# Lp pooling on one core: the blocks of x and out laid out in reverse order of work

## Chip, cores and metric

The kernel runs on one core of one Trainium2 chip; the other cores are idle. The metric is the device time of one launch in microseconds, the median of several runs. A profile is one further execution, taken by the hardware profiler.

## What is computed

The input x is 32 x 256 x 4096 float32 (134.22 MB), p is 2 and the window is 4. Each output element is the root of the mean of four squares that lie side by side, so out is 32 x 256 x 1024 float32 (33.55 MB):

```python
for i in range(length // 4):
    window = np.abs(x[:, :, 4*i:4*i + 4]) ** 2.0
    result[:, :, i] = np.mean(window, axis=-1) ** 0.5
```

A window never crosses the end of a row of x, and windows follow each other without a gap. So x and out can both be read as flat arrays: elements 4j to 4j+3 of x give element j of out, wherever they stand. Any cut of x into pieces whose length is a multiple of 4 gives a cut of out into pieces a quarter as long.

## The kernel before

**Blocks and tiles.** The flat x has 262,144 elements for each of the 128 partitions. This width is cut into 20 tiles (L41 to L47): 18 of 13,184 columns, tile 3 of 13,152, tile 19 of 11,680. The tiles are grouped into six blocks (L51): four of four tiles (0 to 3, 4 to 7, 8 to 11, 12 to 15), one that holds tiles 18, 16, 17 in this order of columns, and one of tile 19 alone. The widths of the blocks are 52,704, three times 52,736, 39,552 and 11,680.

**Where a block lies in memory.** A block is one unbroken stretch of the flat x. Within it, partition 0 owns the first `block_width` elements, partition 1 the next ones, and so on. The function `rows` (L64) computes where the stretch begins (L65), and views it as 128 rows (L66). It is used for x with `div` 1 (in `load`, L83) and for out with `div` 4 (in `store`, L86). With `sum(block_width[:b])`, block 0 is at the front of both arrays and block 5 at their end.

**Loads.** `load(i)` brings tile i, 13,184 columns of all 128 rows of its block, into one of three buffers xt (L58); it is issued by SP. The first three loads go out at the start (L122); load i + 3 goes out once tile i has been summed and its buffer is free (L144).

**Work on a tile.** ACT squares the tile in place (L89). DVE adds columns in pairs (L95) and the pairs into fours (L99), which end in the output tile ot, in PSUM (st), or, for the last tiles, in an xt buffer that is free. ACT takes the roots (L102). For tiles 18 and 19 DVE does a part of the squares (L155). The order of the instructions on each engine is written out by hand (a manual schedule from L62 on, with `ahead` and `behind` in L126 and L127 saying when the roots are taken).

**Stores.** A block is stored by one DMA when all its roots are there. Stores 0, 1 and 2 are issued by ACT (L116), so they have a DMA queue of their own beside the loads; stores 3, 4 and 5 are issued by SP (L147, L168, L172), behind all loads in the queue of the loads.

The functions that the edit touches:

Of the kernel before, what the change touches and what calls it, by code (L numbers as in the profile page):

```python
# [1 line left out]

# [4 lines left out]


@with_exitstack
def kernel(  # L10
    ctx: ExitStack,
    tc: tile.TileContext,
    x: bass.AP,
    p: float,
    kernel_size: int,
    out: bass.AP,
):

    nc = tc.nc

    assert float(p) == 2.0, "kernel specialized for p == 2"
    k = int(kernel_size)  # L30
    assert k == 4, "kernel specialized for kernel_size == 4"

    P = nc.NUM_PARTITIONS
    fp32 = mybir.dt.float32
    Act = mybir.ActivationFunctionType
    add = mybir.AluOpType.add
    xf = x.rearrange("b c l -> (b c l)")
    of = out.rearrange("b c l -> (b c l)")
    total = xf.shape[0] // P

    W = 13184  # L41
    R = W // k
    X_SLOTS = 3
    NARROW = W - 32
    LAST = total - 18 * W - NARROW
    widths = [W] * 3 + [NARROW] + [W] * 15 + [LAST]
    n = len(widths)  # L47
    assert 0 < LAST <= W and LAST % 16 == 0


    blocks = [[0, 1, 2, 3], [4, 5, 6, 7], [8, 9, 10, 11], [12, 13, 14, 15], [18, 16, 17], [19]]  # L51
    block_of = {i: b for b, group in enumerate(blocks) for i in group}
    block_width = [sum(widths[i] for i in group) for group in blocks]

    x_pool = ctx.enter_context(tc.tile_pool(name="x_pool", bufs=1))
    o_pool = ctx.enter_context(tc.tile_pool(name="o_pool", bufs=1))
    s_pool = ctx.enter_context(tc.tile_pool(name="s_pool", bufs=1, space=bass.MemoryType.PSUM))
    x_tiles = [x_pool.tile([P, W], fp32, name=f"xt{j}") for j in range(X_SLOTS)]  # L58
    o_tile = o_pool.tile([P, 4 * R], fp32, name="ot")
    first = o_pool.tile([P, 1], fp32, name="first")  # L60
    s_tile = s_pool.tile([P, 4096], fp32, name="st")
    ctx.enter_context(tc.manual_schedule())  # L62

    def rows(flat, b, div):  # L64
        at = sum(block_width[:b]) * P // div  # L65
        return flat[at:at + block_width[b] * P // div].rearrange("(p w) -> p w", p=P)  # L66


    free = x_tiles[17 % X_SLOTS]
    place = {i: o_tile[:, i % 4 * R:i % 4 * R + widths[i] // k] for i in range(16)}  # L70
    place[18] = free[:, R:2 * R]
    place[19] = free[:, 0:LAST // k]
    place[16] = free[:, 2 * R:3 * R]
    place[17] = free[:, 3 * R:4 * R]
    held = [o_tile[:, 0:w // k] for w in block_width[:4]] + [free[:, R:4 * R], place[19]]

    xs, loads, stores, sums, squares = {}, {}, {}, {}, {}

    def load(i):
        b = block_of[i]  # L80
        at = sum(widths[j] for j in blocks[b][:blocks[b].index(i)])
        xs[i] = x_tiles[i % X_SLOTS][:, 0:widths[i]]
        loads[i] = nc.sync.dma_start(out=xs[i], in_=rows(xf, b, 1)[:, at:at + widths[i]])  # L83

    def store(b, queue):
        stores[b] = queue.dma_start(out=rows(of, b, k), in_=held[b])  # L86

    def square(v):
        return nc.scalar.activation(out=v, in_=v, func=Act.Square)  # L89

    def pairs(v):

        q = v.rearrange("p (n j) -> p n j", j=k)
        h = v[:, 0:v.shape[1] // 2].rearrange("p (n j) -> p n j", j=2)
        return nc.vector.tensor_tensor(out=h, in0=q[:, :, 0:2], in1=q[:, :, 2:4], op=add)  # L95

    def fours(o, v):
        h = v[:, 0:v.shape[1] // 2].rearrange("p (n j) -> p n j", j=2)
        return nc.vector.tensor_tensor(out=o, in0=h[:, :, 0], in1=h[:, :, 1], op=add)  # L99

    def root(o, s):
        return nc.scalar.activation(out=o, in_=s, func=Act.Sqrt, scale=1.0 / k)  # L102

    summed = {i: s_tile[:, 0:R] if i in (4, 8, 12, 16) else place[i] for i in range(n)}

    def roots(*group):
        if len(group) == 1:
            root(place[group[0]], summed[group[0]])
        else:
            v = o_tile[:, group[0] % 4 * R:(group[-1] % 4 + 1) * R]  # L110
            r = root(v, v)
            if group[0] in (5, 9):

                implied(r, stores[block_of[group[0]] - 1])
        if group[-1] in (3, 7, 11):
            store(block_of[group[-1]], nc.scalar)  # L116

    def implied(later, earlier):

        tc.declare_no_dep(later.ins, earlier.ins, reason="implied by the other waits")  # L120

    for i in range(X_SLOTS):  # L122
        load(i)


    ahead = {4: (3,), 8: (7,), 12: (11,)}  # L126
    behind = {3: [(0, 1, 2)], 7: [(5, 6), (4,)], 11: [(9, 10), (8,)], 14: [(12,)], 15: [(13, 14)], 16: [(15,)]}  # L127

    root(first[:, :], nc.const_aps.tensor(1.0, (P, 1), fp32))
    for i in range(17):  # L130
        if i in ahead:
            roots(*ahead[i])
        s = square(xs[i])
        squares[i] = s
        if i == 3:
            implied(s, squares[0])
        if i in (3, 7, 11):

            for earlier in sums[i - X_SLOTS]:
                implied(s, earlier)  # L140
        for group in behind.get(i, []):
            roots(*group)
        sums[i] = pairs(xs[i]), fours(summed[i], xs[i])
        if i + X_SLOTS < n:  # L144
            load(i + X_SLOTS)

    store(3, nc.sync)  # L147
    square(xs[17])
    pairs(xs[17])
    fours(summed[17], xs[17])  # L150
    later = {18: 4608, 19: 2000}

    def shared_square(i):
        v = xs[i][:, 0:later[i]]
        nc.vector.tensor_tensor(out=v, in0=v, in1=v, op=mybir.AluOpType.mult)  # L155
        square(xs[i][:, later[i]:widths[i]])

    def shared_pairs(i):
        implied(pairs(xs[i]), loads[i])

    shared_square(18)
    roots(16)
    roots(17)
    shared_pairs(18)
    fours(summed[18], xs[18])
    shared_square(19)
    roots(18)
    store(4, nc.sync)  # L168
    shared_pairs(19)
    fours(summed[19], xs[19])  # L170
    roots(19)
    store(5, nc.sync)  # L172


# [1 line left out]
_INS = ['x', 'p', 'kernel_size']  # L176
_OUTS = [((32, 256, 1024), 'float32')]

_NUMBERS = {'p': 2.0, 'kernel_size': 4}


# [26 lines left out]
```

## Time and profile before

| what | value |
|---|---|
| median of 3 runs | 393.82 us (393.79, 393.82, 394.0) |
| span of the profiled execution, first to last instruction | 392.3 us |
| median less this span | 1.5 us |
| busy: DVE, ACT, POOL | 218.2, 274.4, 0.2 us |
| moved by DMA | 167.77 MB, mean 428 GB/s over the span |
| one load of 13,184 columns | 6,592 KB, 29.8 us from issue to landing (median of 18) |
| one square (L89) of 13,184 columns | 11.19 us |
| pairs and fours (L95, L99) of such a tile | 7.03 and 3.59 us |

The profile has no total of its own for the profiled execution; its span is the time that a sum can be made against, and what lies around it is taken from the runs. The engines' queues are named ACTq and SPq. DMA q1 is the queue of SP, q10 that of ACT. Beside its page, the trace holds a record for every packet that a DMA engine moved: a packet is here the piece of one partition's row that a load or a store moves, 52,736 bytes in most loads.

### The profile page before, as it was taken

To read this page: it belongs to the slowest core of one execution; us is meant where nothing else is said; L and a number is where in the kernel's file an instruction comes from. 1 tells how busy PE (TensorE), PEld (TensorE's weight loads), DVE (VectorE), ACT (ScalarE), POOL (GpSimd) and SP (SyncE) were. 2 spreads that over 40 slices of the span, in tenths; PEclk is the share of its full clock that TensorE was granted. 3 is DMA by queue.
4 is the path that set the end of the run, shared out by engine and by line. 5 is a ranking of instruction groups with operands and counts; after the bars stand their busy time and mean duration, and the time that the engine had idled before them with its cause. 6 is when DMAs were issued, how large, how long until landed. Compare 5 with 4: busy or idle time off the path is not lost.

```text
span 392.3 us, 176 instructions
## 1 busy us (share of the span) xinstructions
DVE 218.2 (56%) x42; ACT 274.4 (70%) x37; POOL 0.2 (0%) x4
## 2 busy tenths in 40 slices
DVE  0009477580693274905942748069418485699970
ACT  1095695979950859799509597995098999969910
POOL 0000000000000000000000000000000000000000
DMA  8999999999999999999999999999999999999997
GB/s 344 430 430 430 430 440 435 452 457 366 430 430 430 430 430 430 430 441 446 452 446 441 436 430 436 430 430 430 430 430 430 430 430 430 430 453 415 430 413 342
DMA packets 3744, 167.77 MB, mean 428 GB/s; under 512 B 416, under 2 KB 416, under 8 KB 416
## 3 DMA queue, kind: packets, MB, share of 16 engines
q1 hardware_dynamic: 3312, 147.53, 87.4%
q10 hardware_dynamic: 432, 20.25, 11.9%
HBM read 134.22 MB, written 33.55 MB: 428 GB/s over the span
## 4 chain that ended last, share of the span: by engine, by line
DMA 43%; ACT 30%; DVE 23%; issue 0%; ACTq 0%; SPq 0%; DVEq 0%
DMA xt<-in_x_dram 43%; ACT xt L89 28%; DVE xt L95 14%; DVE ot L99 5%; DVE xt L99 3%; DVE xt L155 2%; ACT ot L102 2%; ACT xt L102 1%; ACTq L86 0%; SPq L83 0%; DVEq L95 0%
## 5 line engine op out<-in xcount | busy, mean ns | idle before, releaser
L89 ACT ACTIVATE xt<-xt 128x13184 f32<-128x13184 f32 (+3 forms) x20 | 216.7, 10847 | 92.3 <-DMA xt<-in_x_dram 91.0
L95 DVE TENSOR_TENSOR xt<-xt 128x6592 f32<-128x6592 f32 (+2 forms) x20 | 139.7, 6985 | 144.1 <-ACT xt L89 143.9
L99 DVE TENSOR_TENSOR ot<-xt 128x3296 f32<-128x3296 f32 (+1 forms) x13 | 46.7, 3592 | 17.9 <-DMA out_dram<-ot 17.6
L102 ACT ACTIVATE ot<-ot 128x6592 f32<-128x6592 f32 (+3 forms) x8 | 37.2, 4655 | 7.0 <-DVE ot L99 7.0
L102 ACT ACTIVATE xt<-xt 128x3296 f32<-128x3296 f32 (+1 forms) x3 | 8.5, 2836 | 8.8 <-DVE xt L99 8.8
L99 DVE TENSOR_TENSOR st<-xt 128x3296 f32<-128x3296 f32 x4 | 14.4, 3600 | 0.1
L99 DVE TENSOR_TENSOR xt<-xt 128x3296 f32<-128x3296 f32 (+1 forms) x3 | 10.4, 3461 | 0.1
L102 ACT ACTIVATE ot<-st 128x3296 f32<-128x3296 f32 x3 | 8.7, 2898 | 0.0
L155 DVE TENSOR_TENSOR xt<-xt 128x4608 f32<-128x4608 f32 (+1 forms) x2 | 7.2, 3593 | 0.0
L102 ACT ACTIVATE xt<-st 128x3296 f32<-128x3296 f32 x1 | 2.9, 2898 | 0.0
L102 ACT ACT_TABLE_LOAD x1 | 1.3, 1283 | 0.7 <-PEq L189 0.7
L102 ACT ACTIVATE first<-const-float32-1.0 128x1 f32<-128x1 f32 x1 | 0.2, 202 | 0.0
L189 POOL MEMSET const-bfloat16-1.0<- 128x1 bf16 x1 | 0.1, 101 | 0.0
L189 POOL MEMSET const-uint8-127<- 128x1 uint8 x1 | 0.1, 101 | 0.0
L189 POOL MEMSET const-float32-0.0<- 128x1 f32 x1 | 0.1, 98 | 0.2 <-issue 0.2
L189 POOL MEMSET const-float32-1.0<- 128x1 f32 x1 | 0.1, 98 | 0.0
## 6 DMA issues: line engine op xcount, KB each, us to landing
xt<-in_x_dram SPq DMA_DIRECT2D x18, 6592.0 KB, 29.8
out_dram<-ot ACTq DMA_DIRECT2D x2, 6592.0 KB, 35.1
out_dram<-ot SPq DMA_DIRECT2D x1, 6592.0 KB, 37.1
out_dram<-ot ACTq DMA_DIRECT2D x1, 6588.0 KB, 36.3
xt<-in_x_dram SPq DMA_DIRECT2D x1, 6576.0 KB, 24.7
xt<-in_x_dram SPq DMA_DIRECT2D x1, 5840.0 KB, 21.9
out_dram<-xt SPq DMA_DIRECT2D x1, 4944.0 KB, 16.1
out_dram<-xt SPq DMA_DIRECT2D x1, 1460.0 KB, 8.2
```

The costliest lines, as they stand in the source:

```text
L89: return nc.scalar.activation(out=v, in_=v, func=Act.Square)
L95: return nc.vector.tensor_tensor(out=h, in0=q[:, :, 0:2], in1=q[:, :, 2:4], op=add)
L99: return nc.vector.tensor_tensor(out=o, in0=h[:, :, 0], in1=h[:, :, 1], op=add)
L102: return nc.scalar.activation(out=o, in_=s, func=Act.Sqrt, scale=1.0 / k)
L155: nc.vector.tensor_tensor(out=v, in0=v, in1=v, op=mybir.AluOpType.mult)
L189: nc = _bacc.Bacc("TRN2", target_bir_lowering=False, num_devices=1)
```

## The change

One expression: the start of block b is the sum of the widths of the blocks that are worked after it, not of those before it. As `rows` serves both arrays, x and out are turned round together. Block 5 is now at the front of both, block 0 at their end. Which partition owns which row of a block, the columns of the tiles within a block, the sizes and the order of all instructions stay.

```diff
     def rows(flat, b, div):
-        at = sum(block_width[:b]) * P // div
+        at = sum(block_width[b + 1:]) * P // div
         return flat[at:at + block_width[b] * P // div].rearrange("(p w) -> p w", p=P)
```

## The prediction

> **What bounds the kernel now.** I read the rows of the page on DMA first, since 167.77 MB in 392 us is a lot for one core.
>
> ```profile
> span 392.3 us, 176 instructions
> ...
> DMA  8999999999999999999999999999999999999997
> GB/s 344 430 430 430 430 440 435 452 457 366 430 430 430 430 430 430 430 441 446 452 446 441 436 430 436 430 430 430 430 430 430 430 430 430 430 453 415 430 413 342
> ...
> q1 hardware_dynamic: 3312, 147.53, 87.4%
> q10 hardware_dynamic: 432, 20.25, 11.9%
> ```
>
> The sixteen DMA engines are over 90% busy in every slice but the first and the last, and the two queues together take 99.3% of their time. The waits, for all engines and then for SP's queue alone, show who is slack:
>
> ```profile
> DVE xt L95 <- ACT xt L89: 143.9, 18, 30.0
> ACT xt L89 <- DMA xt<-in_x_dram: 91.0, 13, 16.6
> ```
>
> ```profile
> SPq L83 <- DVE ot L99: 239.4, 13, 38.6
> SPq L83 <- DVE st L99: 91.0, 4, 24.9
> ```
>
> ACT waits 91.0 us for loads; DVE waits mostly for ACT. SP waits long for free buffers, which looks as if compute were late, and in the chain of waits DMA holds only 43%. But a load is issued well before its turn: the load issued at 40.75 us found its predecessor still landing until about 49.9 us (the square of tile 2 starts then), 9 us of cover. So the DMA engines never run dry, and the chain runs through compute only because a load's issue comes after a sum.
>
> To see how even the DMA is, I cut the span into stretches by what moves: loads alone, or loads beside stores 0, 1 and 2 (columns: stretch, length, busy of DVE, ACT and POOL, granted clock, DMA share, GB/s).
>
> ```profile
> 4.30:86.00 81.70, 41.15 (x8) 53.07 (x5) 0.00 (x0) 1.00 1.00 434
> 86.00:94.80 8.80, 1.30 (x1) 7.01 (x2) 0.00 (x0) 1.00 1.01 390
> 94.80:123.90 29.10, 17.65 (x3) 18.20 (x2) 0.00 (x0) 1.00 1.00 433
> 123.90:172.50 48.60, 24.83 (x5) 36.54 (x6) 0.00 (x0) 1.00 1.00 434
> 172.50:201.70 29.20, 17.65 (x3) 19.45 (x2) 0.00 (x0) 1.00 1.00 433
> 201.70:250.30 48.60, 24.83 (x5) 36.53 (x6) 0.00 (x0) 1.00 1.00 434
> 250.30:279.50 29.20, 17.65 (x3) 19.46 (x2) 0.00 (x0) 1.00 1.00 433
> 279.50:345.70 66.20, 38.68 (x8) 55.88 (x7) 0.00 (x0) 1.00 1.00 433
> ```
>
> The rate is 433 to 434 GB/s whether the core only reads or reads and writes, in every block. Only the stretch around 90 us is lower (390). The packet records say why. Packets go in bursts of 16, one on each engine; a packet of 52,736 B takes 1.947 us, with few exceptions. The first burst of the launch has a median of 2.74 us; one burst, at 91.9 us, has 2.87 us (2.61 to 3.11). The latter comes 1.6 us after store 0 was issued:
>
> ```profile
> 87.37 25.63 SPq L83 DMA_DIRECT2D xt<-in_x_dram  x2
> 90.31 0.38 ACTq L86 DMA_DIRECT2D out_dram<-ot  x1
> ```
>
> The whole span by packets, then: 1.74 us until the first packet starts; each engine's 10,485,760 B at 1.947 us per 52,736 B, 387.13 us; the excess of the first burst, 0.72 us; of the stretch from 90 to 100 us, 0.98 us; of all other packets, 0.32 us; 1.35 us from the last data packet to the end. The sum is 392.24, against a span of 392.3. Nothing but DMA stands in it: the last store, issued at 383.2 us, still waits until 386.8 us for the packets of store 4 ahead of it.
>
> **The change, part by part.** It removes and adds no instruction: the lists of the two programs are the same in kind, shape and order on every engine (44 on DVE, 42 on ACT, 25 on SP). The 20 loads and 6 stores keep their issuer, size, rows and pitch; 26 start addresses change.
>
> 1. The issue. An address is a constant of the instruction; 20 issues of 0.33 us on SP and 3 of 0.34 to 0.38 us on ACT stay as they are: 0. The loads that are already queued hide them (the 9 us above); without that cover all 20 would come to 6.6 us.
>
> 2. The shape of packets. In x, blocks 0 to 5 started at 0, 52,704, 105,440, 158,176, 210,912 and 250,464 elements times 128 partitions; now at 209,440, 156,704, 103,968, 51,232, 11,680 and 0 times 128. Every width is a multiple of 32, so every start, old and new, is a multiple of 32 x 128 x 4 = 16,384 B in x and of 4,096 B in out. Rows begin at the same offsets from those starts. So number, size and alignment of packets up to 4 KB stay: 0.
>
> 3. The pace in memory. What no row shows is this block order run backwards. But the trace does show packets at nearly every place of both arrays: six blocks read and six written, one packet per row, rows 210,816 or 210,944 B apart in most of x. If the slightly slower packets from 290 to 360 us (1.948 to 1.955 us, 0.14 us in sum) belong to a place, they move with it, and the sum keeps them. Bounds: these rows, 0.2 us either way. I take 0.
>
> 4. The two slow bursts. The first burst stays the first of its queue; 0.72 us at most could go. The slow burst at 91.9 us is open: it may come with the first write, with the first use of ACT's queue, with a place, or by chance (in the 14 us before it, single packets already took up to 2.14 us). Tied to first use, it stays. From below: it goes, -0.93 (2.87 less 1.947). From above: a second one comes, +0.93. Stores 1 and 2 also entered parts of out that nothing had touched, and their packets took 1.947 us; so did the first loads of blocks 1 to 4. This is the nearest row, and it speaks for a stall of first use. I take 0.
>
> The sum is 0 on a span of 392.3 us. The median of the runs is 1.5 us above that span, for what lies around it, so I forecast 393.8 us. Only a difference over 0.2%, 0.79 us, counts as a change: about what a measurement of this kernel can tell from none.
>
> **The rivals.**
>
> - The stall at 91.9 us goes, because it belonged to the front of out or to that place of x, and nothing replaces it: 393.82 - 0.93 = 392.9. For it: it happens once only. Against it: a burst spreads over the rows of a whole block, so a place in x would be met by many bursts, and the first use of ACT's queue comes after as before.
> - Slower: each large store from ACT stalls all engines once as it starts, because the stores now go down through memory and each opens a place below the last. Stores 1 and 2, which have no such stall, get one each: +1.9, 395.7. One further stall, 0.93 > 0.79, decides. Against it: within a store nothing changes, rows still go up, and each row, 52.7 KB from the next, was opened without a stall in stores 1 and 2.
> - Loads and stores collide in memory. The distance between what is read and what is written beside it changes: while store 0 ran, loads were near the front of x and writes at the front of out; now both are near the end. There are 45 mixed bursts, 15 in each of the three stretches at 433 GB/s. From 0.0175 us per burst on (0.79 / 45) it would be seen. It gives +0.2 us with the excess of the slowest steady bursts (0.004 us), and +42 us, 436, if all went at the pace of the slow one. Against it: three blocks with three distances show no difference (the mixed bursts come every 1.944 us, as do those of loads alone), with the engines and not the memory setting the pace.
>
>  [...]
>
> - That the change doesn't do what it says: both arrays are turned by the one function, so x and out still match; with either order the same bytes move, and the time is that of the forecast.
>
> **How the numbers follow.** No change 0.83 (393.8; its own range 393.5 to 394.2, from the 0.2 us of step 3 and the spread of the runs shown); the stall goes 0.07 (392.9); stalls of further stores 0.08 (395.7, or 394.8 with one); collision 0.02. Faster is the second case, 0.07; slower the last two, 0.10; same 0.83. The range takes in both bounds of step 4: 392.9 to 394.8. It leaves out most of the slower cases, some 1 in 10.
>
> **What would show it.** In the profile after, the same stretches should stand at 433 to 434 GB/s, ACT should wait about 91 us for loads, and one slice near 90 us should still be low. A low stretch near 170 or 250 us would be the stalls of the second rival; a mixed stretch below 430 GB/s the collision; no dip at 90 us the first. I am wrong if the pace of packets of loads alone moves off 1.947 us: then memory has places that are slower, and the trace of before does not show them.

## The result, and the profile after

The changed kernel takes 394.5 us (median of 18 runs, 393.89 to 395.34) against 394.0 us of the kernel before (median of 18 runs, 393.79 to 394.29). The ratio is 1.0014, 95% interval 1.0007 to 1.0020. That is within 0.2%, so it counts as no change by the bound of the prediction, and 394.5 lies in its range of 392.9 to 394.8; but the interval excludes 1, and the median lies outside the 393.5 to 394.2 that the likeliest case gave. So the change costs some 0.5 us, little but clear of the noise, where the prediction had nothing. The scatter has changed more than the median: half of the 18 runs are over 394.5 us, against none of the 18 of before. One run each of e4 and e8 below took over 400 us, in a slower state; the ratios leave these two out, and the profile of e4, which is of such a run, is not used.

The execution that was profiled is one of the shorter ones, 394.16 us with a span of 392.4. Its page answers to that of before line by line:

```profile
span 392.4 us, 176 instructions
...
DMA  8999999999999999999999999999999999999997
GB/s 344 430 430 430 430 434 446 457 430 382 430 430 430 430 441 435 430 446 441 441 441 430 435 446 430 430 430 430 430 430 430 430 430 430 430 448 420 430 437 318
...
q1 hardware_dynamic: 3312, 147.53, 87.3%
q10 hardware_dynamic: 432, 20.25, 11.9%
```

The waits of the engines are the same to 0.1 us in total:

```profile
DVE xt L95 <- ACT xt L89: 144.0, 18, 30.6
ACT xt L89 <- DMA xt<-in_x_dram: 91.0, 13, 17.1
```

So are the stretches, cut where they were cut before (columns: stretch, length, busy of DVE, ACT and POOL, clock, DMA share, GB/s):

```profile
4.30:86.00 81.70, 40.63 (x8) 53.07 (x5) 0.00 (x0) 1.00 1.00 434
86.00:94.80 8.80, 1.81 (x1) 6.50 (x2) 0.00 (x0) 1.00 1.15 461
94.80:123.90 29.10, 17.65 (x3) 18.71 (x2) 0.00 (x0) 1.00 0.96 417
123.90:172.50 48.60, 24.83 (x5) 36.57 (x6) 0.00 (x0) 1.00 1.00 434
172.50:201.70 29.20, 17.65 (x3) 19.42 (x2) 0.00 (x0) 1.00 1.00 433
201.70:250.30 48.60, 24.82 (x5) 36.49 (x6) 0.00 (x0) 1.00 1.00 434
```

The 461 and the 417 are most of one burst of packets, which falls on the other side of the cut at 94.80 (a packet counts where it starts). The slow burst near 92 us is still there, and loads alone still run at 434 GB/s. Only the start differs to the eye. The square of tile 0 waits for all of load 0; before it began at 18.79 us:

```profile
18.79 11.19 ACT L89 ACTIVATE xt<-xt 128x13184 f32<-128x13184 f32 x1 [16.56 <-DMA xt<-in_x_dram]
```

and after, half a microsecond later:

```profile
19.33 11.19 ACT L89 ACTIVATE xt<-xt 128x13184 f32<-128x13184 f32 x1 [17.10 <-DMA xt<-in_x_dram]
```

This half microsecond is not by itself the cost. In e16 below, which takes no longer than before, the square of tile 0 starts as late:

```profile
19.38 11.19 ACT L89 ACTIVATE xt<-xt 128x13184 f32<-128x13184 f32 x1 [17.16 <-DMA xt<-in_x_dram]
```

There all 16 first packets are slow together (3.10 us in the mean, against 2.67 before and 2.80 after).

Tile 0 can be squared when the last engine has done its part of load 0: the square starts 0.02 us after the last of the load's 16 landings in both profiles, though after the change the 15th came 0.18 us before the last. The trace records 16 completions for each DMA of 128 rows (416 packets of 4 bytes for the 26 DMAs, and in e10, where one engine alone moves one DMA more, 417), so it shows how far the engines are apart. For load 0 they span 0.46 us before and 0.93 us after. Each engine has the same share of every DMA (8 of its 128 rows: the packet records of before fall into 16 chains of 208 data packets, for 26 DMAs) and the same pace (1.947 us for 52,736 bytes), so between slow bursts a lag is carried along: 0.47 and 0.87 us at load 4. The slow burst near 92 us changes it, in either direction: behind it, at load 6, the completions span 0.65 and 0.78 us, and those of the last DMA 0.63 and 0.94. In all kernels here, the 16 completions of the last DMA lie 0.4 to 2.6 us apart.

From this came the theory, in two parts: **the time is set by the engine that lags most, not by the mean of the sixteen, and the place of block 0 in x decides how unevenly the engines come off their first packets.** The rivals: the stores (places in out); the direction, down through memory instead of up; two copies of a program differing by chance.

### The profile page after: what moved, and what is told of

Same layout as the page of the kernel before. It is cut to its first block, busy times and chain, and to the rows that moved or that the text cites. A ratio compares the mean times of both kernels' runs of the same rounds, so it can differ in the third digit from the quotient of the medians.

```text
span 392.4 us, 176 instructions
## 1 busy us (share of the span) xinstructions
DVE 218.2 (56%) x42; ACT 274.4 (70%) x37; POOL 0.2 (0%) x4
## 4 chain that ended last, share of the span: by engine, by line
DMA 43%; ACT 30%; DVE 23%; issue 0%; ACTq 0%; SPq 0%; DVEq 0%
DMA xt<-in_x_dram 43%; ACT xt L89 28%; DVE xt L95 14%; DVE ot L99 5%; DVE xt L99 3%; DVE xt L155 2%; ACT ot L102 2%; ACT xt L102 1%; ACTq L86 0%; SPq L83 0%; DVEq L95 0%
```

## Experiments

Each experiment was measured beside the kernel before, on the same chip. The table puts the runs together; "spread" is the distance of the 16 completions of load 0 in the one profile, "lag" that of the last completion of all from the mean of its 16. Ratios are to before, of means.

| kernel | start of block 0 in x, bytes | median us | ratio (95%) | runs over 394.5 | spread | lag |
|---|---|---|---|---|---|---|
| before | 0 | 394.0 | | 0 of 18 | 0.46 | 0.39 |
| e1_control | 0 | 393.98 | 0.9997 (0.9989 to 1.0006) | 0 of 11 | 0.70 | 0.28 |
| e3_out_only | 0 | 394.02 | 1.0001 (0.9993 to 1.0010) | 0 of 11 | 0.77 | 0.42 |
| e16_rest_reversed | 0 | 394.03 | 1.0001 (0.9992 to 1.0010) | 0 of 11 | 0.69 | 0.34 |
| e6_last_at_front | 5,980,160 | 393.97 | 1.0001 (0.9992 to 1.0009) | 0 of 11 | 0.82 | 0.41 |
| e7_big_four_down | 81,002,496 | 393.99 | 0.9999 (0.9990 to 1.0008) | 0 of 11 | 0.59 | 0.22 |
| e12_first_near_end | 101,253,120 | 393.97 | 0.9998 (0.9989 to 1.0007) | 0 of 11 | 0.69 | 0.13 |
| the changed kernel | 107,233,280 | 394.5 | 1.0014 (1.0007 to 1.0020) | 9 of 18 | 0.93 | 0.53 |
| e4_after_again | 107,233,280 | 394.93 | 1.0023 (1.0006 to 1.0040) | 8 of 13 | | |
| e8_after_third | 107,233,280 | 394.56 | 1.0019 (1.0004 to 1.0034) | 7 of 11 | 1.00 | 1.53 |
| e9_after_warm | 107,233,280 | 394.55 | 1.0015 (1.0006 to 1.0024) | 6 of 11 | 1.07 | 0.52 |
| e2_x_only | 107,233,280 | 394.23 | 1.0023 (1.0004 to 1.0042) | 4 of 11 | 0.95 | 0.47 |
| e5_first_at_end | 107,233,280 | 394.17 | 1.0014 (1.0000 to 1.0028) | 2 of 11 | 1.03 | 0.30 |
| e13_same_phase | 98,844,672 | 394.39 | 1.0013 (1.0004 to 1.0021) | 3 of 11 | 0.82 | 0.48 |
| e18_start_16k | 16,384 | 395.32 | 1.0031 (1.0017 to 1.0044) | 7 of 10 | 1.18 | 2.03 |
| e14_tile0_at_end, load 0 alone, rows 52,736 bytes apart | 127,467,520 | 394.1 | 1.0003 (0.9995 to 1.0012) | 0 of 11 | 0.65 | 0.55 |
| e15_tile0_at_front, load 0 alone, rows 52,736 bytes apart | 0 | 394.74 | 1.0017 (1.0008 to 1.0025) | 8 of 11 | 0.95 | 0.77 |
| e10_one_engine_late | 0 | 394.71 | 1.0024 (1.0011 to 1.0037) | 12 of 12 | 0.46 | 1.13 |

A profile is one execution; the runs are the evidence, the profiles tell what the lag does. Medians and counts are over all runs. The ratios, being of means, are moved by single runs of 397 to 398.4 us, which e2 (two), e4, e5, e8, e10 and e18 (one each) have. Beside these kernels, 4 of 157 runs of before were over 394.5, the longest 395.08.

### x alone, out alone, the copy, and the change once more

e1_control is the kernel before. e2_x_only and e3_out_only turn one array:

```diff
-        at = sum(block_width[:b]) * P // div
+        at = sum(block_width[b + 1:] if div == 1 else block_width[:b]) * P // div
```

(and the other way round for out).

> The kernel before, run as if it were a changed one: what two copies of one program differ by. If the +0.14% of the reversed blocks is only how one loaded copy of a program stands to another (theory: copies), this copy too may lie 0.05% to 0.15% off. If it is the places in memory (theory: places), it lies within 0.03% of 394.0 us, with runs no further apart than before's (393.8 to 394.3).

> Only x lies in reverse order of work, out as before (so the output's blocks are not those of the reference; sizes and instructions stay). Theory loads (the first burst of loads is stalled longer and more unevenly where block 0 lies at the end of x: 0.85 us mean excess in the profile after, 0.72 before): +0.3 to +0.6 us with runs up to 395.3, and a first burst with packets over 3.1 us. Theory stores (the stall at store 0 depends on where in out it writes): as before, 394.0, runs within 0.5 us.

> Only out lies in reverse order of work, x as before (output's blocks not those of the reference). Theory loads: as before, 394.0, runs within 0.5 us. Theory stores: +0.3 to +0.6 us with runs up to 395.3, and the slow burst near 92 us longer than 2.9 us or met twice.

> The changed kernel again, for its scatter and a second profile. All theories of places: 394.3 to 394.7 median, runs from 393.9 to 395.3. Theory copies: it may come out anywhere within 0.15% of before, with a narrow scatter too. The second profile tells whether the excess of the first burst (0.85) and of the slow burst (0.86 in 90 to 100 us) move from one execution to the next.

Measured: the copy gives 0.9997 and out alone 1.0001, with no run over 394.5 us. x alone gives 1.0023, the changed kernel 1.0023. So the copies theory and the stores theory fall, and the loads are left. The changed kernel's scatter is a property of it. How much of it x alone has is less clear than the equal ratios say: that of x alone rests on two runs of 397.01 and 398.15 us (without them its mean is 1.0007 of before's), and its median, 394.23, is below the +0.3 us that was expected, while the changed kernel's, 394.93, is above its 394.3 to 394.7.

### Which block, and is it direction, shift or the first block?

Three other orders of the blocks in both arrays, by a list in place of the sum:

```diff
-        at = sum(block_width[:b]) * P // div
+        laid = [1, 2, 3, 4, 5, 0]
+        at = sum(block_width[j] for j in laid[:laid.index(b)]) * P // div
```

(e6: `[5, 0, 1, 2, 3, 4]`; e7: `[3, 2, 1, 0, 4, 5]`; e8 is the changed kernel.)

> x and out both in the order 1, 2, 3, 4, 5, 0: only the block worked first is at the far end, the others go up through memory. So far out turned alone gave 394.02 us, x turned alone 394.23 with single runs up to 398.2, both turned 394.5 and 394.9 with runs up to 395.4 and two beyond. Theory first (the launch's first loads meet a place at the end of x): median 394.3 to 394.9, runs above 394.6 in a third of the cases. Theories direction and shift: shift, some (all starts but one moved, to other 16 KB phases); direction, none: 394.0, nearly all runs below 394.4.

> Order 5, 0, 1, 2, 3, 4: the small last block at the front, so that blocks 0 to 4 go up as before but begin 5,980,160 bytes later, at the odd 16 KB phase that they have in the changed kernel. Theory shift (where the block starts lie against a larger power of two decides how rows read in step share memory): 394.3 to 394.9 with runs up to 395.3. Theory direction (loads that go down from block to block): 394.0. Theory first: 394.0.

> Order 3, 2, 1, 0, 4, 5: the four large blocks go down, the two last stay where they were; starts of the four are multiples of 64 KB. Theory direction: 394.3 to 394.9 with runs up to 395.3. Theory shift: 394.0. Theory first: 394.0 to 394.2, as block 0 is not at the end, though far from the front.

> The changed kernel a third time, beside the three orders on the same chip: 394.3 to 394.9 median, a third of the runs or more above 394.6, if its scatter is a property of it. If it comes out at 394.0 with no run above 394.5, the scatter belongs to the chip or the hour and not to the layout.

Measured: the two orders without block 0 at the end are at 393.97 and 393.99 us with no run over 394.3; direction falls, and so does shift in the form it was put; that rows read in step share memory, which it supposed, no run here shows. Block 0 alone at the end (e5) gives 1.0014 (1.0000 to 1.0028), less than was expected: two runs of 11 over 394.5.

The profile of e8 is a longer execution, 395.11 us, and shows where the microsecond went. Its packets take no longer than those of before: the excess over the steady pace is 1.98 us per engine, against 2.02. But one engine lags. The end of before and of e8 in short stretches (last columns: DMA share, GB/s); first before,

```profile
390.00:391.00 1.00, 0.00 (x0) 0.00 (x0) 0.00 (x0) 1.00 0.32 129
391.00:392.00 1.00, 0.00 (x0) 0.00 (x0) 0.00 (x0) 1.00 0.00 0
```

then e8, whose line of waits for loads follows:

```profile
390.00:391.00 1.00, 0.00 (x0) 0.00 (x0) 0.00 (x0) 1.00 0.18 70
391.00:392.00 1.00, 0.00 (x0) 0.00 (x0) 0.00 (x0) 1.00 0.06 23
```

```profile
ACT xt L89 <- DMA xt<-in_x_dram: 92.0, 13, 17.0
```

A share of 0.06 is one engine in sixteen: fifteen have finished, earlier than before (0.18 against 0.32), and the last one works alone for another microsecond. Loads that land late by one engine make ACT wait, so the total of its waits is a microsecond longer too, 92.0 us against 91.0, though nothing on the path of ACT has changed.

### Is a lagging engine enough, and can it be healed?

e10 leaves the blocks where they were before, and gives one engine a packet more, behind load 2. e9 (the changed kernel) and e11 (before) try to take the first meeting with the rows away from load 0, by a small load on ACT's queue:

```diff
+    nc.scalar.dma_start(out=warm[:, :], in_=rows(xf, 0, 1)[:, 0:128])
     for i in range(X_SLOTS):
         load(i)
```

```diff
     for i in range(X_SLOTS):
         load(i)
+    late = xf[0:6584].rearrange("(p w) -> p w", p=1)
+    nc.sync.dma_start(out=o_tile[0:1, 2 * R:2 * R + 6584], in_=late)
```

e12 is the order `[1, 2, 3, 4, 0, 5]`.

> The kernel before (block 0 at the front), and one DMA of a single partition's row, 26,336 bytes, behind load 2, which one engine alone moves: at 27.1 bytes per ns it is 0.97 us of work. Nothing else changes. Theory spread (every engine has its eighth of each DMA's rows, none is slack, so the latest engine sets the end): +0.6 to +1.0 us, 394.6 to 395.0, although the work is 1/16 of that per engine on average (0.06 us). If a wide spread also breeds further stalls, runs up to 395.5 and beyond appear, as in the changed kernel. Rival (work is evened out over the engines or later waits absorb it): 394.0 to 394.1.

> The changed kernel, with one more small load at the start: the first 512 bytes of each row of block 0, issued by ACT on its own queue, beside load 0. In the profiles so far, the 16 engines' completions of load 0 lie 0.93 to 1.03 us apart where block 0 of x is at the end, and 0.46 to 0.82 us where it is not, and the distance lasts to the end. Theory spread (the first meeting with the rows at the end of x is slow and uneven; the engine that comes off worst sets the end): the small load takes the uneven meeting on itself or beside it; if that evens the engines, spread of load 0 below 0.8 us and median 394.0 to 394.2 without runs above 394.6. If the place is slow whatever was read before: 394.5 and more as now. Beside it: if the slow burst near 92 us is the first use of ACT's queue, it goes here (0.9 us less); if it is the first write to out, it stays.

> The kernel before with the same small load at the start as the other kernel has: its control. If the slow burst near 92 us is the first use of ACT's queue, 0.9 us less, 393.1; if it is the first write, 394.0. If the small load costs start time, +0.1 to +0.4 us.

> Order 1, 2, 3, 4, 0, 5: block 0 near the end of x but 5,980,160 bytes lower than in the changed kernel, and on a multiple of 64 KB. Theory place (the last part of x is what meets the first loads badly): as with block 0 at the very end, median 394.15 to 394.3 with a run or two above 394.9, spread of load 0 over 0.9 us. Rival (the exact start 107,233,280 matters, by its phase): 394.0, no run above 394.4, spread of load 0 below 0.82 us.

Measured: one packet on one engine (0.976 us in the trace) makes the kernel 394.71 us, ratio 1.0024 (1.0011 to 1.0037), with all 12 runs over 394.5. Spread over 16 engines the same bytes would be, as an estimate, 0.06 us (0.976 / 16). (The expectation speaks of an eighth of each DMA's rows; it is eight of the 128 rows, a sixteenth.) A small DMA more is not the reason: e11 adds a larger one, 64 KB spread over all 16 engines, and takes 0.20 us more (1.0005, 0.9997 to 1.0014). This is the first part of the theory, and it holds without any change of place. That 0.64 us (394.71 less 394.07) come of 0.976 fits, as an estimate, an engine that was not the last before: the last one of before is 0.39 us behind the mean. The end of its profile has the same mark, one engine alone (a share of 0.03 in a microsecond is one engine for half of it):

```profile
390.00:391.00 1.00, 0.00 (x0) 0.00 (x0) 0.00 (x0) 1.00 0.12 47
391.00:392.00 1.00, 0.00 (x0) 0.00 (x0) 0.00 (x0) 1.00 0.03 12
```

The warm-up misses its aim: the trace shows the small packets from 4.2 us on, each engine taking its first one after its first packet of load 0. So load 0 still met the rows first, and e9 (394.55, like the change) tells nothing of healing. e11 tells something else: the queue of ACT had been used long before, and the slow burst near 92 us was still there (excess in 90 to 100 us: 1.13 us).

e12 was the surprise. Block 0 near the end, only 5,980,160 bytes lower, is as good as before: 0.9998, no run over 394.3. So "near the end of x" is not the reason.

### The last part of x, or the phase of the start?

For this, block 0 of x can be read from anywhere; block 0 of out is then made of other elements, by the same instructions. e13 reads it 8 MiB below its place in the change, e18 from byte 16,384; e16 is the change with block 0 of x read from the front. e14 and e15 read load 0 alone as one unbroken piece at the end or at the front.

```diff
+        at = sum(block_width[:b]) * P // div if div != 1 or b else (107233280 - 8 * 2 ** 20) // 4
```

(e18: `16384 // 4`; e16: the changed sum, and 0.)

```diff
+        if i == 0:
+            part = xf[(total - W) * P:total * P].rearrange("(p w) -> p w", p=P)
```

(e15: `xf[0:W * P]`.)

> The kernel before, but block 0 of x is read from byte 98,844,672, 8 MiB lower than where it lies in the changed kernel: the same phase against every power of two up to 8 MiB, and not the last part of x (it reads a stretch that other blocks read too, so the output's block 0 is another). Theory phase: spread of load 0 at 0.9 us or more, median 394.15 or more with runs above 394.9. Theory last part of x: spread below 0.82 us, 394.0, no run above 394.4.

> The kernel before, but load 0 alone reads the last 6,750,208 bytes of x as one unbroken piece (row after row, so all engines' first packets fall in that part; tile 0's output is another). Theory last part: the first burst is slower than the 2.7 us of the other kernels or its spread above 0.9 us, and the median above 394.15. Theory phase: as the run with load 0 unbroken at the front.

> The control: load 0 alone reads the first 6,750,208 bytes of x as one unbroken piece (tile 0's output is another). Rows lie 52,736 bytes apart here instead of 210,816. Both theories: spread of load 0 at 0.5 to 0.8 us, 394.0, as before, if the pitch of the first load's rows is of no account.

> The changed kernel, but block 0 of x is read from the front, where it lies in the kernel before (the output's block 0 is another); blocks 1 to 5 of x and all of out stay reversed. Theory first block: 394.0, no run above 394.4, spread of load 0 below 0.82 us. Rival (the reversed order of the rest costs by itself): 394.2 to 394.5 with runs above 394.9, at an ordinary spread of load 0.

> The kernel before, but block 0 of x is read from byte 16,384 on (the output's block 0 is another). Start 107,233,280 of the changed kernel and 98,844,672 of the run 8 MiB lower are both 16,384 above a multiple of 262,144; the four starts without effect (0, 5,980,160, 81,002,496, 101,253,120) are not. Theory low part (the start modulo 262,144 counts): median 394.2 or more, runs above 394.5. Rival (higher parts of the address count): 394.0, no run above 394.4.

Measured: the same phase 8 MiB lower has the effect, 394.39 us, 1.0013 (1.0004 to 1.0021), runs up to 395.15; its spread in the one profile is 0.82 only, where 0.9 was expected, but that profile is of a short run, 394.10. Load 0 wholly in the last part of x has none: 394.10, 1.0003 (0.9995 to 1.0012). So it is not the last part of x. The control e15 missed what both theories said: unbroken at the front it takes 394.74 us, 1.0017 (1.0008 to 1.0025), spread 0.95. Its start is 0, but its rows lie 52,736 bytes apart instead of 210,816. So the pitch of the first load's rows (the distance from one row to the next) counts as well as its start.

e16 settles the other half: with all of out and blocks 1 to 5 of x reversed, and block 0 of x at the front, 394.03 us, 1.0001, no run over 394.4. So the cost of the change needs its addresses of block 0 in x; the reversed rest alone costs nothing.

e18 starts at 16,384 and costs more than the change itself: 395.32 us, 1.0031 (1.0017 to 1.0044), seven of ten runs over 395. Its profile, of a run of 395.79 us, shows the lag most clearly. The page's span, and its waits for loads:

```profile
span 394.0 us, 176 instructions
```

```profile
ACT xt L89 <- DMA xt<-in_x_dram: 92.7, 13, 17.2
```

The packets again take no longer in sum than before: an excess of 2.05 us per engine, against 2.02. The lag does it, and it grows in steps. From the completions of the loads in the trace, the distance of the last engine from the last but one:

```
load                    0     3     6     8     12    14    19    last store
last behind 15th, us    0.38  0.38  1.27  1.27  1.32  1.86  1.74  1.74
```

It comes with load 0, and grows by 0.9 us between loads 3 and 6, when store 0 starts, and by 0.5 us between 12 and 14, when store 2 starts; between, it is carried. It is one engine throughout. In this trace each packet starts as another ends, so the records fall into 16 chains of 208 packets, 10,485,760 bytes each. The last engine's first packet starts at 2.63 us, 0.62 us after the mean, and takes 2.82 us; its slow packet near 92 us takes 3.41 us (the others' 2.39 to 3.22); and it alone has three more packets that take longer than the pace, 2.28 us at 102.19, 2.28 at 250.33 and 2.09 at 264.33. The profile of e8 shows the same two steps (0.05, then 0.61, then 1.37). At the end fifteen engines are done and one works on into the last microsecond:

```profile
391.00:392.00 1.00, 0.00 (x0) 0.00 (x0) 0.00 (x0) 1.00 0.06 23
392.00:393.00 1.00, 0.00 (x0) 0.00 (x0) 0.00 (x0) 1.00 0.03 12
```

But the step at the slow burst goes either way. In e5 load 0 has a spread of 1.03 us, and the last engine is 0.65 us behind the mean at load 4; after the burst it is 0.30, and so to the end. Over the 15 profiles of kernels with no DMA added, the lag behind the burst (load 6) goes with the span more closely (correlation 0.97) than the spread of load 0 does (0.71, and 0.45 without e8 and e18). So the second part of the theory is shown only as far as this: the place of block 0 costs time, and the kernels that pay have a spread of load 0 of 0.82 us or more, the others of 0.82 us or less. That the cost comes through this spread is argued.

### The slow burst near 92 us

e17 adds to e11 a store of the small tile, to the place of block 0 in out:

```diff
+    nc.scalar.dma_start(out=rows(of, 0, k)[:, 0:128], in_=warm[:, :])
```

> The kernel before with a small load at the start, as in the kernel that warms it (394.27, its slow burst stays at 1.13 us in 90 to 100 us), and a store of these 64 KB to the place of block 0 in out, which store 0 later overwrites. Theory first write (the slow burst is what the first write of a launch to out costs): the excess in 90 to 100 us falls below 0.2 us, and a like excess appears within the first 15 us, where it costs the same: 394.1 to 394.4. Rival (it belongs to the large store, or to the turn from loads alone to loads beside stores): the excess of 0.8 to 1.1 us stays near 92 us.

Measured: the small store's packets are moved between 19.5 and 39 us, later than the expectation had them, and no large packet beside them takes over 1.97 us; the excess in 90 to 100 us is 0.89 us, against 1.13 in e11 and 0.98 before. So the burst is neither the first use of ACT's queue (e11) nor the first write of the launch. That it belongs to the start of the first large store, or to the time of 92 us, is left open; for the store speaks that an engine's slow packet is nearly always the last load packet or the last but one before its first packet of store 0 (in 298 of 304 chains of packets, 16 in each of 19 profiles). The kernel takes 394.53 us against 394.02: each engine moves 16 packets more, at 0.027 us 0.43 us of it. (e11 has 8 of them, 0.22 us, and measured 394.27 against 394.07.)

## Why the prediction was right, and where it failed

**What bounds the kernel.** Right: the DMA engines have no gap (the two queues take 99.2% of their time after the change, 99.3% before), and ACT's wait for loads, 91.0 us, did not move. **The sum of the span** was made of the wrong thing. I added the mean time of the packets of the 16 engines, 389.15 us, to the first start, and met the span. The agreement was partly luck: 1.74 and 389.15 make 390.89, where the last engine ends (390.91 us in that profile), while the mean engine, whose packets were added, ends at 390.51. Over 15 profiles (before, after and all experiments that add no DMA, without e4) the span goes with the lag of the last engine (correlation 0.97) and hardly with the mean excess (0.25). Without the two longest, e8 and e18, it goes with both (0.89 and 0.79).

**Step 1**, the issue: right; an issue still takes 0.33 us on SP (median) and 0.34 to 0.38 us on ACT. **Step 2**, the packets: "number, size and alignment of packets up to 4 KB stay: 0" is true and was not enough. This is the step that failed: of the 26 start addresses that change it asked only whether packets are aligned as before up to 4 KB, and put the rest at 0. The runs show some 0.5 us in its place, and that those of block 0 in x, which the launch's first loads read, are needed for it: reversing all else costs nothing (e16, 1.0001), moving these alone, to two other starts of the same phase, costs (e13, 1.0013; e18, 1.0031). What in the addresses counts is known in part. The phase against larger powers of two (the start modulo such a power) did change. The three starts with the effect are 16,384 above a multiple of 262,144; of the four without it none is. Modulo 65,536 one of the four (5,980,160) is like the three, modulo 131,072 none is; so it takes at least the part of the address up to 131,072 to tell them apart. This is a rule read off seven starts, of which e13 and e18 were foretold by it, and it is not the only thing that counts: e15 pays at phase 0 with another pitch, and e18 has more than twice the cost of e13 at the same phase, though the intervals touch.

**Step 3**, the pace: right. The steady pace is 1.947 us in both profiles. The slightly slower packets from 290 to 360 us did not move with their place, as I thought that they might: they sum to 0.14 us per engine in the same stretch after the change, so in these two orders they go with the order of the work and not with addresses.

**Step 4**, the two slow bursts: I priced the first burst by its mean alone ("0.72 us at most could go") and saw no way for it to cost more. Its mean did move little, 0.72 to 0.85 us, and the control has 0.79. Its unevenness went from 0.46 to 0.93 us; the profile of before is a low one here, as the control has 0.70 and the other kernels without the cost up to 0.82. The slow burst at 92 us stayed, as taken, but it too leaves the engines uneven (0.65 and 0.78 us at load 6), and the step priced it only as 0.93 us more or less for all 16 together.

**The rivals.** None came. The nearest was the collision of loads and stores: the lagging engine did lose further time where a store starts beside loads (0.9 and 0.5 us in e18, some 0.6 and 0.8 in e8), but for one engine, not for all 45 mixed bursts, and turning out costs nothing (e3 and e16, 1.0001 each). The mixed stretches went at 417, 433 and 433 GB/s after the change, the first without most of the burst that fell ahead of its cut. That the engines and not the memory set the pace was read off equal paces (a mixed burst every 1.944 us, as without stores); no run here separates the two.

**The numbers.** "No change" held by the bound of 0.79 us, and 394.5 lies below 394.8; but that is luck, since the upper end was made of a second slow burst of 0.93 us, which did not come. Of the 0.7 us between the forecast and the median, 0.2 is the base, 393.82 from three runs against 394.0 from 18. The median's +0.5 us is not in the likeliest case's own range, since its 0.2 us took the spread of three runs of before for that of the changed kernel.

What stays open: how the start of the rows makes the engines uneven (no run here separates memory from the way to it, and where x itself lies in memory is not on record); why the same start gives medians of 394.2 us with the other blocks or out forward (e5, e2) and 394.5 to 394.9 with all reversed, with intervals that overlap; and why a lag grows or shrinks when a store starts. No version here beats the kernel before: the best orders (e12, e7) are level with it.

## What to carry to other kernels

When a kernel keeps all DMA engines busy from end to end, as this one does (99.3% of their time before), account for it by the last engine, not by the mean: in e10, 0.976 us more on one engine cost 0.64 us. With 8 of the 128 rows of every DMA on each engine, the steady stretches changed a lag by some 0.2 us at most here; the slow burst near 92 us made it smaller in e5 (from 0.65 us behind the mean to 0.30) and larger in e18 (from 0.38 us behind the last but one to 1.27). Changes of layout that keep sizes, counts and alignment up to 4 KB still moved this kernel by 0.1% to 0.3% (1.0014 in the change, 1.0013 in e13, 1.0031 in e18), through the addresses of the first loads, so read the scatter of the runs and not only the median. An unexplained cost is worth splitting by array and by block before a mechanism is named: here turning out alone, four blocks alone and a last block moved to the front took three stories off the list.

## What was not expected of the hardware

- The first packet of each engine took 1.9 to 3.5 us in the profiles here (2.01 to 3.00 before, 2.31 to 3.42 after), in the mean some 2.6 to 3.1, instead of 1.947, and how unevenly went with where the first load's rows start and with their pitch (spread of load 0: 0.46 to 0.82 us in the kernels without the effect, 0.82 to 1.18 us with it).
- In every kernel here the packets near 92 us were slow on nearly all engines (in sum 0.7 to 1.2 us per engine more than the pace, in the mean; 0.98 before, 0.86 after, 1.13 in e11, 0.89 in e17), whether or not ACT's queue or out had been used before.
- A load of 64 KB in packets of 512 B, issued on ACT's queue beside load 0, took 18.7 us to land (e17): its packets take 0.027 us, but each engine moved one of them only after each 52,736-byte packet of the other queue, 1.967 us apart.
